# Recurrent layer's opening in a two-layer flow-matching step: two small products tied into the first units' product order, weight splits behind them, pool waits tile by tile, state copies on GpSimd

## Chip, cores, metric

One core of a Trainium2 chip runs the whole kernel. Its engines work beside each other, each through its own list of instructions in order: TensorE (PE, matrix products into PSUM), VectorE (DVE), ScalarE (ACT), GpSimd (POOL) and SyncE (SP, which only issues transfers). An instruction may wait for a semaphore that another engine raises; everything behind it on its engine then waits too. The metric is the device time of one launch in microseconds, median over runs.

## What is computed

Two layers over 512 latent and 128 context tokens of width 1024, in fp32. Layer 0 mixes by attention, layer 1 by a bidirectional gated linear recurrence; each is followed by a SwiGLU FFN. Each sub-layer has an RMS norm, a shift and scale from the conditioning vector, and a gated residual. The recurrent mixer is

```python
gate, xr = jnp.split(xm @ w_in, 2, axis=-1)
xc = _centred_depthwise_conv(xr, conv_w, conv_b)          # width 4
r = sigmoid(xc @ w_a + b_a); i = sigmoid(xc @ w_i + b_i)  # block diagonal, 8 blocks of 128, each direction
log_a = -LRU_C * r * softplus(-lam)
a, b = exp(log_a), sqrt(-expm1(2.0 * log_a)) * (i * xc)
h[t] = a[t] * h[t-1] + b[t]                               # forward and backward; latents start from state_h
y = (hs_f + hs_b) * gelu(gate)
return y @ w_out, jnp.stack([hT_f, hT_b], axis=1)         # context's last states are an output
```

with `xm = norm(x) * (1 + scale) + shift` per token.

## The kernel before

**Tiling.** Activations lie feature-major: 8 tiles of 128 features by 640 tokens. Each value and weight is split into a high part (the matmul format) and a low rest, and every product is done as three: hi·hi, hi·lo, lo·hi (L213, L214, L215). A unit is one 128-feature column of a weight. `unit` loads it to `raw` (SP, L167), makes the high part `whi` and the low part `wlo` (the split on DVE, L182). In the recurrent layer `whi` is loaded a second time by a GpSimd transfer (L178) that converts it; elsewhere ACT casts it (L180). `chunk` does one unit's 24 products (8 of k, three each) for a stretch of tokens, into a PSUM bank with the tag `mm`, of which there are three.

**Stages.** Modulation columns and first norm; attention; `ffn0` (output projection, FFN of layer 0, ending in `project_closing`); `lru`; `ffn1`. Each stage is a `phase`, which opens a pool of SBUF tiles and one of PSUM tiles in the memory that the last stage's pools held. In what order the instructions of one engine stand is decided when the program is built: a scheduler takes the program in order of writing and moves instructions within what data and buffers allow. `issue_after` ties an instruction behind another one.

**The end of ffn0.** `project_closing` does the FFN's down projection for tokens 0:384 (first chunk) of all features, then 384:640 (second chunk). Each is added to x (L436, DVE), squared (L375, ACT) and summed (L377, DVE; `self.sq` is the last). `moment` sums over the features with products against ones (L389, L392, tile `at`, per block of 128 tokens), DVE takes the variance (L394), GpSimd the power −1/2 (L396), DVE spreads it on a diagonal `dg` (L398). `spread` turns `dg` into the row factor of all partitions (L406, tile `rr`). `modulate` makes the normed input: `nv` (L411, DVE), its high part (L412, ACT), its low part (L413, DVE), tile `big`. For the first chunk this is done beside the second chunk's products, for the second chunk at the stage's end, in eight tiles.

**The recurrent layer.** Weight columns f = 0 to 7 give xr, others the gates. The opening loads x0, g0 and x1 (unit f = 0 of xr and of the gate, and unit 1 of xr) and does their first chunks, then x0's second: `x0[0], g0[0], x1[0], x0[1], g0[1]`. ACT copies xr out of PSUM (L1001); as there are three banks, x0's second chunk waits for the copies of its first. Then, in a loop over t that works on several units at once: `lru_a` does the convolution (L1009 on ACT, three L1011 on DVE), the gate products `gp` (L1021, PE), tanh (L1022, ACT) and L1023; `lru_b` does L1029, the exponential and tanh (L1033, L1034), the square root (L1035, ACT), and L1036 and L1037 (DVE); `lru_c` does four scans (L1046, DVE; two for each direction), copies the last context state out of each direction into `st` (L1048, ACT), and adds the directions (L1053, L1054); `lru_d` multiplies with the gate (L1058) and splits the result (L1062 on ACT, L1063 on DVE). The gate's unit goes through L1071, L1073 and L1075 (ACT). At the end SP writes `st` to the output `nh`.

Of the kernel before, what the change touches and what calls it, by code (L numbers as in the profile page):

```python
# [17 lines left out]
KT = D // P  # L18
# [4 lines left out]
CHL = ((0, 384), (384, 640))  # L23
# [98 lines left out]
def _pieces(t0, t1):  # L122
    return [(s, max(a, t0), min(b, t1)) for s, a, b in ((0, 0, NLAT), (1, NLAT, NTOK)) if max(a, t0) < min(b, t1)]


class _Step:
# [23 lines left out]

    @contextmanager
    def phase(self, name, **tags):
        with self.tc.tile_pool(name="ps" + name, bufs=1, space=bass.MemoryType.PSUM) as self.pp, \
                self.tc.tile_pool(name=name, bufs=1) as self.sb:
            self.wx, self.quota = [tags.pop(t, 0) for t in ("wx", "quota")]
            self.ptags, self.pbufs, self.share = list(tags), tags, True
            yield self.sb
# [45 lines left out]
                t1 = NTOK  # L203
            evac(t0, slice(t0, t1), ps[:, 0:t1 - t0])

    def chunk(self, u, xhi, xlo, t0, t1, mx=True):
        nc = self.nc
        hi, lo = u
        nk = hi.shape[1]
        ps = self.pg(mx)[:, :t1 - t0]  # L210
        s = slice(t0, t1)
        for k in range(nk):
            nc.tensor.matmul(ps, hi[:, k], xhi[:, k, s], start=(k == 0), stop=False)  # L213
            nc.tensor.matmul(ps, hi[:, k], xlo[:, k, s], start=False, stop=False)  # L214
            nc.tensor.matmul(ps, lo[:, k], xhi[:, k, s], start=False, stop=(k == nk - 1))  # L215
        return ps
# [237 lines left out]
    def project_closing(self, w, hi, lo, gk, key, nh, nl, xd):  # L454
        G = self.need(self.gcols, gk)
        A, B = [self.need(self.AB, key + (j,)) for j in range(2)]
        us = []

        def out(f, t0, t1):
            self.residual(f, t0, t1, self.chunk(us[f], hi, lo, t0, t1), G, True)  # L460
            self.nc.sync.dma_start(xd[f * P:f * P + P, t0:t1], self.x[:, f, t0:t1])

        def normed(k, t0, t1):
            v = self.t([P, 384], F32, "nv", 3, self.sb)
            for s, a, b in _pieces(t0, t1):
                self.modulate(k, a, b, A[:, s, k:k + 1], B[:, s, k:k + 1], v[:, a - t0:b - t0], nh, nl)
        for f in range(KT):
            us.append(self.unit(w[f]))
            for c, (t0, t1) in enumerate(CHL):
                if c == 0 or f < KT - DEH:  # L470
                    out(f, t0, t1)
        for c, (t0, t1) in enumerate(CHL):
            for f in range(KT - DEH, KT) if c else ():
                out(f, t0, t1)
                j = f - KT + DEH
                for k in range(max(0, 2 * j - 2), 2 * j) if f < KT - 1 else ():
                    normed(k, *CHL[0])
            self.stat(t0, t1)
        for k in range(KT):
            normed(k, *CHL[1])  # L480
# [253 lines left out]
    def normed(self, k, t0, t1, key):  # L734
        nc = self.nc
        A, B = [self.need(self.AB, key + (j,)) for j in range(2)]
        for s, a, b in _pieces(t0, t1):
            v = self.x[:, k, a:b]
            nc.vector.scalar_tensor_tensor(v, v, A[:, s, k:k + 1], self.rt[:, a:b], ALU.mult, ALU.mult)
            nc.scalar.activation(v, v, AF.Identity, bias=B[:, s, k:k + 1])  # L740
# [244 lines left out]
        c = CI["ba0"] * KT  # L985
        nc.vector.tensor_scalar(self.hb, self.cols[:, c:c + 4 * KT], 0.5, None, ALU.mult)

    def halves(self, w, hi, lo, ev):
        u = self.unit(w)
        return [lambda t0=t0, t1=t1: ev(t0, self.chunk(u, hi, lo, t0, t1)) for t0, t1 in CHL]  # L990

    def lru_xr(self, f, hi, lo):
        xr = self.xrs[f % 2]
        nat = xr[:, 2:514].rearrange("p (r c) -> p c r", r=ROWS)

        def ev(t0, ps):
            for o, a, b, r in ((nat[:, 56:64], 0, 64, ROWS), (nat[:, 0:40], 64, 384, ROWS),
                               (nat[:, 40:56], 384, 512, ROWS), (xr[:, 517:645], 512, 640, 0)):
                if t0 <= a and b <= t0 + 384:
                    v = ps[:, a - t0:b - t0]  # L1000
                    self.nc.scalar.copy(o, v.rearrange("p (c r) -> p c r", r=r) if r else v)  # L1001
        return self.halves(self.i["wi"][KT + f], hi, lo, ev)

    def lru_a(self, f, lp):
        nc, xr = self.nc, self.xrs[f % 2]
# [34 lines left out]
    def lru_c(self, f, a, h):  # L1040
        nc = self.nc
        for d in range(2):
            st = self.st[:, d * KT + f:d * KT + f + 1]
            for sl, init in ((slice(0, NLAT), self.col(f"h{d}", f)), (slice(C0, LW), 0.0)):
                hv, av = [t[:, d, sl] if d == 0 else t[:, d, sl][:, ::-1] for t in (h, a)]
                nc.vector.tensor_tensor_scan(hv, av, hv, init, ALU.mult, ALU.add)  # L1046
            e = LW - 1 if d == 0 else C0
            nc.scalar.copy(st, h[:, d, e:e + 1])  # L1048
# [13 lines left out]
        self.nc.scalar.copy(hi, v)  # L1062
        self.nc.vector.tensor_tensor(lo, v, hi.bitcast(F32), ALU.subtract)  # L1063

    def lru_gate(self, f, hi, lo, lp):
# [10 lines left out]
        return G, self.halves(self.i["wi"][f], hi, lo, ev)  # L1076

    def new_x(self, st):
        pool = st.enter_context(self.tc.tile_pool(name="x", bufs=1))
        self.x = self.t([P, KT, NTOK], F32, "x", 1, pool)  # L1080

    def load_x(self, src):
# [3 lines left out]
    def run(self):  # L1086
        nc, tc, i, o = self.nc, self.tc, self.i, self.o
# [19 lines left out]
        xhi = self.big()  # L1107
        xlo = self.big()
# [38 lines left out]
        xhi = self.big(n=NTOK + 2)  # L1147
        xlo = self.big(n=NTOK + 2)
# [12 lines left out]
        xhi, xlo = self.nh, self.nl  # L1161
# [3 lines left out]
        with self.phase("lru", at=1) as lp:  # L1165
            A, B, C, G = {}, {}, {}, {}
            self.xrs = [self.t([P, 648], F32, f"xr{j}", 1, lp) for j in range(2)]
            for xr in self.xrs:
                for a, b in ((0, 2), (514, 517), (645, 648)):
                    nc.gpsimd.memset(xr[:, a:b], 0.0)  # L1170

            def gate(g):
                G[g], halves = self.lru_gate(g, xhi, xlo, lp)
# [54 lines left out]
```

## Time and profile before

| | us |
|---|---|
| median of three runs | 1554.61 |
| lowest, highest | 1553.47, 1556.66 |
| the profiled execution, whole | 1557.38 |
| its span in the trace | 1555.6 |
| its mean granted TensorE clock | 0.988 of full |
| DVE, ACT, POOL busy | 1059.7, 698.2, 216.9 |

How rows are read: a row of a timeline has the start, the duration in us, the engine, the line, the operation, output<-input with their shapes, the count of instructions put together, and in brackets the idle time of the engine before it and what ended it. Instructions of one engine overlap a little, so durations sum to more than the time between starts. A row of windows has the stretch and its length, then the busy time of PE, PE's weight loads, DVE, ACT and POOL (each with its instructions), the granted clock of TensorE, the share of the transfer engines, and GB/s. A row of the waits has the waiting engine and line, what ended the wait, the sum, the number and the longest.

### The profile page before, as it was taken

To read this page: it belongs to the slowest core of one execution; us is meant where nothing else is said; L and a number is where in the kernel's file an instruction comes from. 1 tells how busy PE (TensorE), PEld (TensorE's weight loads), DVE (VectorE), ACT (ScalarE), POOL (GpSimd) and SP (SyncE) were. 2 spreads that over 40 slices of the span, in tenths; PEclk is the share of its full clock that TensorE was granted. 3 is DMA by queue.
4 is the path that set the end of the run, shared out by engine and by line. 5 is a ranking of instruction groups with operands and counts; after the bars stand their busy time and mean duration, and the time that the engine had idled before them with its cause. 6 is when DMAs were issued, how large, how long until landed. Compare 5 with 4: busy or idle time off the path is not lost. (4 is left out here: it accounts for less than half of the span.)

```text
span 1555.6 us, 26009 instructions
## 1 busy us (share of the span) xinstructions
PE 1491.8 (96%) x10309; PEld 1444.3 (93%) x10309; DVE 1059.7 (68%) x2000; ACT 698.2 (45%) x1282; POOL 216.9 (14%) x253
## 2 busy tenths in 40 slices
PE   6999999989999999999999799979999999999997
PEld 4899899879999999999999787779999999999996
DVE  5668788949999997434444669874875666555656
ACT  4576667655333123312332378762734342524242
POOL 2101122100111110000000000000222222222210
PEclk9999999999999999999999899999999999999998
DMA  9445656536666664222223343315242322222211
GB/s 376 146 126 158 176 159 183 145 106 190 190 191 190 191 215 130 61 82 82 68 71 101 104 153 95 115 55 200 86 136 72 92 82 81 84 79 83 81 55 68
DMA packets 73210, 196.65 MB, mean 126 GB/s; under 512 B 8176, under 2 KB 25728, under 8 KB 72960
## 3 DMA queue, kind: packets, MB, share of 16 engines
q1 hardware_dynamic: 58976, 144.49, 29.8%
q0 software_dynamic: 13824, 50.34, 10.7%
q8 instruction: 81, 1.33, 0.4%
q14 instruction: 41, 0.34, 0.1%
q10 hardware_dynamic: 288, 0.16, 0.0%
HBM read 179.48 MB, written 8.92 MB: 121 GB/s over the span
## 5 line engine op out<-in xcount | busy, mean ns | idle before, releaser
L213 PE MATMUL mm<-big,whi 128*128 128x320 f32 (+3 forms) x1290 | 402.4, 315 | 21.3 <-ACT xr L1001 9.4
L214 PE MATMUL mm<-big,whi 128*128 128x320 f32 (+3 forms) x1290 | 404.8, 314 | 0.7 <-DVE big L1063 0.4
L215 PE MATMUL mm<-big,wlo 128*128 128x320 f32 (+3 forms) x1290 | 404.0, 314 | 0.7 <-DVE wlo L182 0.7
L213 PEld LDWEIGHTS mm<-big,whi 128*128 128x128 f32 x1290 | 245.9, 192 | 26.2 <-ACT xr L1001 9.6
L214 PEld LDWEIGHTS mm<-big,whi 128*128 128x128 f32 x1290 | 247.0, 191 | 4.0 <-DVE big L1063 2.5
L215 PEld LDWEIGHTS mm<-big,wlo 128*128 128x128 f32 x1290 | 246.7, 191 | 2.2 <-DVE wlo L182 1.1
L243 DVE SCALAR_TENSOR_TENSOR mprod<-mraw,csb 128x1024 f32<-128x1024 f32 x160 | 196.2, 1226 | 13.9 <-DMA mraw<-in_wm 13.6
L436 DVE SCALAR_TENSOR_TENSOR x<-mm,G,x 128x128 f32<-128x128 f32 (+3 forms) x211 | 85.6, 436 | 94.0 <-PE mm L215 93.3
L182 DVE TENSOR_TENSOR wlo<-raw,whi 128x1024 fp32r<-128x1024 f32 (+1 forms) x90 | 110.1, 1223 | 29.8 <-ACT whi L180 21.6
L180 ACT CAST whi<-raw 128x1024 fp32r<-128x1024 f32 (+1 forms) x74 | 76.7, 1036 | 108.1 <-PE mm L214 66.5
L213 PE MATMUL mm<-big,whx 128*128 128x320 f32 (+3 forms) x363 | 113.3, 312 | 0.0
L215 PE MATMUL mm<-big,wlx 128*128 128x320 f32 (+3 forms) x363 | 113.0, 311 | 0.0
L214 PE MATMUL mm<-big,whx 128*128 128x320 f32 (+3 forms) x363 | 112.7, 311 | 0.0
L239 POOL DMA_DIRECT2D mraw<-in_wm x80 | 43.5, 544 | 385.8 <-DVE mprod L243 269.4
L213 PE MATMUL mx<-big,whi 128*128 128x320 f32 (+3 forms) x278 | 86.5, 311 | 0.9 <-DVE big L686 0.9
L214 PE MATMUL mx<-big,whi 128*128 128x320 f32 (+3 forms) x278 | 86.3, 310 | 0.0
L215 PE MATMUL mx<-big,wlo 128*128 128x320 f32 (+3 forms) x278 | 86.3, 310 | 0.0
L180 ACT CAST whx<-raw 128x1024 fp32r<-128x1024 f32 (+1 forms) x40 | 41.0, 1028 | 92.6 <-PE mm L214 55.1
L213 PE MATMUL mx<-big,whx 128*128 128x320 f32 (+3 forms) x245 | 76.0, 310 | 0.0
L215 PE MATMUL mx<-big,wlx 128*128 128x320 f32 (+3 forms) x245 | 75.7, 309 | 0.0
L214 PE MATMUL mx<-big,whx 128*128 128x320 f32 (+3 forms) x245 | 75.4, 308 | 0.0
L1062 ACT CAST whi<-raw 128x1024 fp32r<-128x1024 f32 (+1 forms) x41 | 41.4, 1009 | 72.3 <-PE mm L214 45.0
(294 smaller groups left out, 3573.5 us busy)
## 6 DMA issues: line engine op xcount, KB each, us to landing
raw<-in_gu SPq DMA_DIRECT2D x88, 512.0 KB, 3.6
mraw<-in_wm POOLq DMA_DIRECT2D x80, 512.0 KB, 4.0
raw<-in_dn SPq DMA_DIRECT2D x24, 512.0 KB, 3.7
raw<-in_wqk SPq DMA_DIRECT2D x16, 512.0 KB, 4.9
raw<-in_wi SPq DMA_DIRECT2D x16, 512.0 KB, 3.6
whi<-in_wi POOLq DMA_DIRECT2D x16, 512.0 KB, 4.1
raw<-in_dn SPq DMA_DIRECT2D x16, 448.0 KB, 3.3
sw<-in_wm SPq DMA_DIRECT2D x10, 512.0 KB, 10.6
```

The lines of the kernel that those rows point to most:

```text
L180: nc.scalar.copy(hi, raw)
L182: nc.vector.tensor_tensor(lo, raw, hi.bitcast(F32), ALU.subtract)
L213: nc.tensor.matmul(ps, hi[:, k], xhi[:, k, s], start=(k == 0), stop=False)
L214: nc.tensor.matmul(ps, hi[:, k], xlo[:, k, s], start=False, stop=False)
L215: nc.tensor.matmul(ps, lo[:, k], xhi[:, k, s], start=False, stop=(k == nk - 1))
L239: nc.gpsimd.dma_start(w, self.i["wm"][l * 6 + j - 2, f])
L243: nc.vector.scalar_tensor_tensor(prod, w, 1.0, self.csb[:, s], ALU.mult, ALU.mult, accum_out=out[:, s, f:f + 1])
L436: self.nc.vector.scalar_tensor_tensor(xs, ps[:, a - t0:b - t0], G[:, s, f:f + 1], xs, ALU.mult, ALU.add)
L1062: self.nc.scalar.copy(hi, v)
```

## The change

The two phase pools and the pool of x are opened with `reuse_waits="tile"`: a tile placed in the memory of an earlier pool waits for the tiles that lay in its own place, and not for the whole earlier pool. In the recurrent layer's opening the products of x0's first chunk from k = 3 on are tied behind the last `at` product, and g0's first product behind the last `rr` product. The low split of g0 is tied behind the last sum of squares, that of x1 behind `dg`. Two norm tiles (k = 6 and 7 of the first chunk) stand behind the last feature's residual, and are tied behind the last sum. The state copies go from ACT to GpSimd, the output transfer of the states from SP to GpSimd.

```diff
-        with self.tc.tile_pool(name="ps" + name, bufs=1, space=bass.MemoryType.PSUM) as self.pp, \
-                self.tc.tile_pool(name=name, bufs=1) as self.sb:
+        with self.tc.tile_pool(name="ps" + name, bufs=1, space=bass.MemoryType.PSUM, reuse_waits="tile") as self.pp, \
+                self.tc.tile_pool(name=name, bufs=1, reuse_waits="tile") as self.sb:
...
+    def pin(self, ins):
+        return self.tc.issue_after(ins) if ins is not None else nullcontext()
...
+    def chunk(self, u, xhi, xlo, t0, t1, mx=True, pins={}):
...
         for k in range(nk):
-            nc.tensor.matmul(ps, hi[:, k], xhi[:, k, s], start=(k == 0), stop=False)
+            with self.pin(pins.get(k)):
+                nc.tensor.matmul(ps, hi[:, k], xhi[:, k, s], start=(k == 0), stop=False)
...
         def normed(k, t0, t1):
             v = self.t([P, 384], F32, "nv", 3, self.sb)
-            for s, a, b in _pieces(t0, t1):
-                self.modulate(k, a, b, A[:, s, k:k + 1], B[:, s, k:k + 1], v[:, a - t0:b - t0], nh, nl)
+            with self.pin(self.sq if t0 == 0 and k > 5 else None):
+                for s, a, b in _pieces(t0, t1):
+                    self.modulate(k, a, b, A[:, s, k:k + 1], B[:, s, k:k + 1], v[:, a - t0:b - t0], nh, nl)
...
-                for k in range(max(0, 2 * j - 2), 2 * j) if f < KT - 1 else ():
+                for k in range(max(0, 2 * j - 2), 2 * j) if f < KT - 2 else ():
                     normed(k, *CHL[0])
+            for k in (6, 7) if c else ():
+                normed(k, *CHL[0])
             self.stat(t0, t1)
...
-    def halves(self, w, hi, lo, ev):
-        u = self.unit(w)
+    def halves(self, w, hi, lo, ev, after=None):
+        u = self.unit(w, None, after)
...
-            nc.scalar.copy(st, h[:, d, e:e + 1])
+            nc.gpsimd.tensor_copy(st, h[:, d, e:e + 1])
...
-        pool = st.enter_context(self.tc.tile_pool(name="x", bufs=1))
+        pool = st.enter_context(self.tc.tile_pool(name="x", bufs=1, reuse_waits="tile"))
...
-            x0, g0, x1 = self.lru_xr(0, xhi, xlo), gate(0), self.lru_xr(1, xhi, xlo)
-            for step in (x0[0], g0[0], x1[0], x0[1], g0[1]):
+            x0, g0, x1 = self.lru_xr(0, xhi, xlo), gate(0, self.sq), self.lru_xr(1, xhi, xlo, self.dg)
+            x0[0](pins={3: self.at})
+            g0[0](pins={0: self.rr})
+            for step in (x1[0], x0[1], g0[1]):
                 step()
...
-            nc.sync.dma_start(o["nh"], self.st)
+            nc.gpsimd.dma_start(o["nh"], self.st)
```

(`lru_xr` and `lru_gate` take the argument `after` too and hand it to `halves`.) The names in the listings below have numbers that tell one tile from the next of its kind.

On PE, around the product `rr`: before, at the end of x1's first chunk (mm_1616) and ahead of x0's second (mm_1617):

```order
L213 MATMUL mm_1616_9567<-big_1517_8871,whi_1612_9510 128x384
L214 MATMUL mm_1616_9567<-big_1518_8872,whi_1612_9510 128x384
L215 MATMUL mm_1616_9567<-big_1517_8871,wlo_1613_9511 128x384
L406 MATMUL rr_1591_9416<-dg_1590_9414,ones_5_72 128x128 x2
L213 MATMUL mm_1617_9594<-big_1517_8871,whi_1605_9497 128x256
```

and now, at the end of x0's first chunk (mm_1614) and ahead of g0's first (mm_1615):

```order
L217 MATMUL mm_1614_9514<-big_1517_8871,whi_1605_9497 128x384
L218 MATMUL mm_1614_9514<-big_1518_8872,whi_1605_9497 128x384
L219 MATMUL mm_1614_9514<-big_1517_8871,wlo_1606_9498 128x384
L410 MATMUL rr_1591_9416<-dg_1590_9414,ones_5_72 128x128 x2
L217 MATMUL mm_1615_9541<-big_1517_8871,whi_1609_9504 128x384
```

So `rr` went from behind three first chunks to behind one; the four `at` products stand behind k = 2 of x0's first chunk now, and stood behind all of g0's before.

On DVE, the end of the first norm chunk and the chain to `dg` (ssq is the sum of squares, wlo_1610 the low split of g0, wlo_1613 that of x1, big_1518 the low part of the normed input). Before, the split of g0 stands some rows ahead of these:

```order
L413 SCALAR_TENSOR_TENSOR big_1518_8872<-nv_1579_9334,B10_1108_5975,big_1517_8871 128x384
L182 TENSOR_TENSOR wlo_1613_9511<-raw_1611_9508,whi_1612_9510 128x1024
L413 SCALAR_TENSOR_TENSOR big_1518_8872<-nv_1580_9338,B10_1108_5975,big_1517_8871 128x384
L377 TENSOR_TENSOR ssq_1523_8902<-ssq_1523_8902,sq_1582_9366 128x256
L411 SCALAR_TENSOR_TENSOR nv_1583_9370<-x_863_4082,A10_1023_5343,rr_1566_9202 128x384
L411 SCALAR_TENSOR_TENSOR nv_1584_9374<-x_863_4082,A10_1023_5343,rr_1566_9202 128x384
L413 SCALAR_TENSOR_TENSOR big_1518_8872<-nv_1583_9370,B10_1108_5975,big_1517_8871 128x384
L413 SCALAR_TENSOR_TENSOR big_1518_8872<-nv_1584_9374,B10_1108_5975,big_1517_8871 128x384
L394 TENSOR_SCALAR var_1588_9410<-at_1587_9405 128x2
L398 TENSOR_TENSOR dg_1590_9414<-ident_2_63,rs_1589_9412 128x256
```

and now:

```order
L417 SCALAR_TENSOR_TENSOR big_1518_8872<-nv_1580_9338,B10_1108_5975,big_1517_8871 128x384
L381 TENSOR_TENSOR ssq_1523_8902<-ssq_1523_8902,sq_1582_9366 128x256
L415 SCALAR_TENSOR_TENSOR nv_1585_9397<-x_863_4082,A10_1023_5343,rr_1566_9202 128x384
L182 TENSOR_TENSOR wlo_1610_9505<-raw_1608_9502,whi_1609_9504 128x1024
L415 SCALAR_TENSOR_TENSOR nv_1586_9401<-x_863_4082,A10_1023_5343,rr_1566_9202 128x384
L398 TENSOR_SCALAR var_1588_9410<-at_1587_9405 128x2
L417 SCALAR_TENSOR_TENSOR big_1518_8872<-nv_1585_9397,B10_1108_5975,big_1517_8871 128x384
L417 SCALAR_TENSOR_TENSOR big_1518_8872<-nv_1586_9401,B10_1108_5975,big_1517_8871 128x384
L402 TENSOR_TENSOR dg_1590_9414<-ident_2_63,rs_1589_9412 128x256
L182 TENSOR_TENSOR wlo_1613_9511<-raw_1611_9508,whi_1612_9510 128x1024
```

Both splits went from ahead of the last sum to behind it, and the variance from behind the last two low parts to ahead of them.

On GpSimd, in the middle of the recurrent layer, the loads of the converted weights (`whi`). Before, they follow one another:

```order
L178 DMA whi_1685_10098<-in_wi 128x1024
L178 DMA whi_1692_10177<-in_wi 128x1024
L178 DMA whi_1705_10265<-in_wi 128x1024
L178 DMA whi_1712_10344<-in_wi 128x1024
L178 DMA whi_1725_10432<-in_wi 128x1024
L178 DMA whi_1732_10511<-in_wi 128x1024
L178 DMA whi_1747_10618<-in_wi 128x1024
L178 DMA whi_1754_10699<-in_wi 128x1024
```

and now the state copies (lt are the scans' tiles) stand between them:

```order
L1055 COPY st_6_74<-lt_1631_9709 128x1 x2
L178 DMA whi_1712_10344<-in_wi 128x1024
L1055 COPY st_6_74<-lt_1645_9804 128x1 x2
L178 DMA whi_1725_10432<-in_wi 128x1024
L1055 COPY st_6_74<-lt_1659_9911 128x1
L178 DMA whi_1732_10511<-in_wi 128x1024
L1055 COPY st_6_74<-lt_1659_9911 128x1
L178 DMA whi_1747_10618<-in_wi 128x1024
L1055 COPY st_6_74<-lt_1679_10078 128x1 x2
L178 DMA whi_1754_10699<-in_wi 128x1024
```

More of the change, by code (lines that the diff above doesn't have):

```diff
@@ L986, in lru_prep, with lru_xr @@
         nc.vector.tensor_scalar(self.hb, self.cols[:, c:c + 4 * KT], 0.5, None, ALU.mult)
-    def halves(self, w, hi, lo, ev):
-        u = self.unit(w)
-        return [lambda t0=t0, t1=t1: ev(t0, self.chunk(u, hi, lo, t0, t1)) for t0, t1 in CHL]
-    def lru_xr(self, f, hi, lo):
+    def halves(self, w, hi, lo, ev, after=None):
+        u = self.unit(w, None, after)
+        return [lambda t0=t0, t1=t1, **kw: ev(t0, self.chunk(u, hi, lo, t0, t1, **kw)) for t0, t1 in CHL]
+    def lru_xr(self, f, hi, lo, after=None):
         xr = self.xrs[f % 2]
@@ L1001, in ev @@
                     self.nc.scalar.copy(o, v.rearrange("p (c r) -> p c r", r=r) if r else v)
-        return self.halves(self.i["wi"][KT + f], hi, lo, ev)
+        return self.halves(self.i["wi"][KT + f], hi, lo, ev, after)
     def lru_a(self, f, lp):
@@ L1063, in split, with lru_gate @@
         self.nc.vector.tensor_tensor(lo, v, hi.bitcast(F32), ALU.subtract)
-    def lru_gate(self, f, hi, lo, lp):
+    def lru_gate(self, f, hi, lo, lp, after=None):
         nc = self.nc
@@ L1170, in run, with gate @@
                     nc.gpsimd.memset(xr[:, a:b], 0.0)
[L1172 to L1176 removed]
+            def gate(g, after=None):
+                G[g], halves = self.lru_gate(g, xhi, xlo, lp, after)
+                return halves
+            x0, g0, x1 = self.lru_xr(0, xhi, xlo), gate(0, self.sq), self.lru_xr(1, xhi, xlo, self.dg)
+            x0[0](pins={3: self.at})
+            g0[0](pins={0: self.rr})
+            for step in (x1[0], x0[1], g0[1]):
                 step()
```

3 lines of the change are left out of this document (1 added, 2 removed).

## The prediction

> **What bounds the kernel now.** I read the page first (busy shares, costliest groups), then TensorE's waits by releaser, then the windows and the timelines around the long waits. Times are of the one profiled execution: span 1555.6 us, 1557.38 us in all, 0.2% over the median of 1554.61.
>
> ```profile
> PE 1491.8 (96%) x10309; PEld 1444.3 (93%) x10309; DVE 1059.7 (68%) x2000; ACT 698.2 (45%) x1282; POOL 216.9 (14%) x253
> ```
> ```profile
> PE mm L213 <- ACT xr L1001: 9.4, 1, 9.4
> PE mm L213 <- ACT big L1062: 7.4, 3, 6.3
> ```
>
> PE is the bound: 1555.6 − 1491.8 = 64 us of the span are idle, and no more than that (and any slow clock) can be won without removing products, of which the change removes none. The first row (total, number of waits, longest) is at the opening of the recurrent layer, where x0's second chunk (256 tokens) waits 9.4 us. Of the second, 6.3 us are at that layer's end.
>
> ```profile
> 858.78 0.28 PE L215 MATMUL mm<-big,wlx 128*128 128x256 f32 x1
> ...
> 860.56 0.28 PE L215 MATMUL mm<-big,wlx 128*128 128x256 f32 x1
> 860.68 0.34 PE L213 MATMUL mm<-big,whi 128*128 128x384 f32 x1
> ...
> 874.26 0.61 PE L406 MATMUL rr<-dg,ones 128*128 128x128 f32 x4
> 884.27 0.58 PE L213 MATMUL mm<-big,whi 128*128 128x256 f32 x1 [9.40 <-ACT xr L1001]
> ```
> ```profile
> 875.00:884.00 9.00, 0.00 (x0) 0.00 (x0) 8.33 (x32) 5.92 (x18) 0.27 (x6) 0.70 0.00 0
> 884.00:889.00 5.00, 4.73 (x23) 4.73 (x24) 0.00 (x0) 1.27 (x4) 0.00 (x0) 0.52 0.29 107
> ```
>
> The wait is paid twice: the granted clock (third number from the end) falls to 0.70 in the gap and stays at 0.52 while x0's second chunk runs. Before the gap PE did three first chunks (x0, g0, x1) back to back from 860.68, and rr only behind them, at 874.26. The second chunk's norm hangs on rr:
>
> ```profile
> 864.89 0.42 DVE L377 TENSOR_TENSOR ssq<-ssq,sq 128x256 f32<-128x256 f32 x1
> ...
> 866.52 1.15 DVE L413 SCALAR_TENSOR_TENSOR big<-nv,B,big 128x384 fp32r<-128x384 f32 x2 [0.16 <-ACT big L412]
> 870.10 0.16 DVE L394 TENSOR_SCALAR var<-at 128x2 f32<-128x2 f32 x1 [2.43 <-PE at L392]
> 871.15 0.42 DVE L398 TENSOR_TENSOR dg<-ident,rs 128x256 f32<-128x256 f32 x1 [0.90 <-POOL rs L396]
> 874.90 1.64 DVE L411 SCALAR_TENSOR_TENSOR nv<-x,A,rr 128x128 f32<-128x128 f32 x6 [3.33 <-PE rr L406]
> ...
> 882.20 1.13 DVE L413 SCALAR_TENSOR_TENSOR big<-nv,B,big 128x128 fp32r<-128x128 f32 x4
> ```
> ```profile
> 881.27 1.47 ACT L412 ACTIVATE big<-nv,B 128x128 fp32r<-128x128 f32 x4 [0.87 <-DVE nv L411]
> 883.40 0.81 ACT L1001 COPY xr<-mm 128x64 f32<-128x64 f32 x2 [0.66 <-DVE big L413]
> ...
> 889.43 0.50 ACT L1001 COPY xr<-mm 128x128 f32<-128x128 f32 x2 [4.16 <-PE mm L215]
> ```
> ```profile
> 870.41 0.71 POOL L396 TENSOR_TENSOR rs<-var,mhalf 128x2 f32<-128x2 f32 x1 [11.09 <-DVE var L394]
> 883.44 0.27 POOL L1170 MEMSET xr<- 128x2 f32 x6 [12.31 <-DVE big L413]
> ```
>
> DVE waits 2.43 us for the at products and 3.33 us for rr, which stand behind other units in PE's queue though their data were there. Then eight tiles of norm, to 883.3, and only then the first xr copies: x0's first chunk lies finished in its PSUM bank since 865, but the copy's wait, like the memset's, ends with the last L413.
>
> **The change, part 1: the opening.** By the new order the g0 split no longer stands ahead of the last sum of squares, and the x1 split stands behind dg. A split holds DVE 1.14 us, so the sum of 864.89 ends near 862.6 (f = 6's square is there by 862.3). PE does k = 0 to 2 of x0 (nine products of 0.175 us from 860.68, to 862.25), waits some 0.4 us, does at in 0.8 us, and then k = 3 to 7 (15 × 0.175 = 2.6 us) to 866.1 or a little later, since the low parts for k = 6 and 7 now end near 866.1. Beside that DVE does two nv, the g0 split between them, var at 864.8, GpSimd the power (0.71 us) to 865.8, DVE two low parts (1.15 us), dg to 866.5. rr runs at 866.7, ending at 867.3. DVE uses the time for the x1 split (866.5 to 867.65), so the eight tiles start at 867.65 instead of 874.90: **7.25 us earlier**, at their old 8.4 us. ACT's last L412 (882.74 before) ends near 875.5, and the copies start there rather than after memset and last L413: 0.6 us more. x0's second chunk starts at 884.27 − 7.9 = 876.3.
>
> What is late next? PE has g0's and x1's first chunks as cover: 48 × 0.175 = 8.4 us from 867.3, to 875.6. A gap of 0.7 us is left. Whether the clock drops in it is read from other gaps:
>
> ```profile
> 986.40:988.60 2.20, 0.12 (x1) 0.00 (x0) 2.20 (x3) 1.93 (x3) 0.00 (x0) 1.00 0.00 0
> 988.60:990.60 2.00, 1.99 (x6) 1.09 (x7) 2.00 (x2) 1.27 (x4) 0.00 (x0) 1.00 0.00 0
> ```
> ```profile
> 1047.40 0.90 PE L213 MATMUL mm<-big,whi 128*128 128x320 f32 x2 [6.27 <-ACT big L1062]
> ```
> ```profile
> 1047.40:1051.00 3.60, 3.60 (x13) 3.51 (x14) 2.44 (x3) 2.66 (x3) 0.00 (x0) 0.50 0.19 37
> ```
>
> After 2.1 us without products the clock is still 1.00; after 6.27 us it is 0.50. So with gaps under 1 us it should hold. The chunk took 5.1 us (884.27 to the copies at 889.43); at the pitch of the 256-wide products before the gap (1.78 us for 15, 0.119 each) 24 take 2.85. I take 2.0 us of the difference. Opening: −7.9 − 2.0 = **−9.9 us**, between −7.9 (the clock falls all the same) and −10.5. It carries through, since xc of unit 0 and all scans follow x0's second chunk.
>
> The Trainium skill, "TensorE: Matmul & The Clock Gate", section "What's actually happening", gives half clock after an idle window of about 3.4 us, and full clock after as long a busy one, the window running freely. By that rule a gap of 0.7 us leaves the clock alone, and the two rows above agree; the sum would be the same, and if the gap were several microseconds some 2 us less.
>
> **Part 2: the state copies.** Sixteen copies of one column each leave ACT for GpSimd.
>
> ```profile
> L1048 ACT COPY st<-lt x16: 177/192/216, 932.6 to 1042.2; 128x1 f32<-128x1 f32 x16
> its engine sat idle before it (us, times) until:
>   DVE lt L1046: 14.8, 11
> ```
> ```profile
> 925.00:979.00 54.00, 51.28 (x299) 43.98 (x298) 52.93 (x63) 46.57 (x70) 3.26 (x5) 1.00 0.37 115
> ```
> ```profile
> 974.33 0.19 ACT L1048 COPY st<-lt 128x1 f32<-128x1 f32 x1 [2.04 <-DVE lt L1046]
> 975.83 0.19 ACT L1048 COPY st<-lt 128x1 f32<-128x1 f32 x1 [1.30 <-DVE lt L1046]
> ```
> ```profile
> 971.83 1.24 PE L1021 MATMUL gp<-xc,gw 128*128 128x512 f32 x4
> ```
> ```profile
> 986.26 1.50 DVE L1036 SCALAR_TENSOR_TENSOR lt<-lt,lt 128x1286 f32<-128x1286 f32 x1 [1.36 <-ACT lt L1035]
> ...
> 1006.19 1.50 DVE L1036 SCALAR_TENSOR_TENSOR lt<-lt,lt 128x1286 f32<-128x1286 f32 x1 [2.26 <-ACT lt L1035]
> ...
> 1028.55 2.91 DVE L1036 SCALAR_TENSOR_TENSOR lt<-lt,lt 128x1286 f32<-128x1286 f32 x2 [1.77 <-ACT lt L1035]
> ```
>
> ACT stands 14.8 us in these waits for a scan, with tanh, exp and square root queued behind. Until 979 that costs nothing: DVE is busy 52.93 of 54 us and is the bound. After it DVE waits for ACT's square root (L1035) each round. Walking ACT's queue without the copies: the tanh held up behind the pair at 974 and 975 starts when its gate product is there (971.83 + 1.24 = 973.07) and not behind the second copy, at 975.92, so L1035 and the L1036 of 986.26 come 2.85 us earlier; the next pair (994, 995) lets the L1036 of 1006.19 come 4.85 us earlier, the pair at 1011 and 1013 the one of 1028.55 6.3 us. From there DVE runs without a gap to 1047, so the layer's last values, for which PE waits 6.27 us up to 1047.40, move as a whole. I take **−6.0**, between 0 and −6.5.
>
> A copy's price on GpSimd isn't in this trace. The nearest rows are a memset (0.27 us for six) and the power (0.71 us), so 16 cost 0.7 to 11 us of an engine that is 14% busy. What queues behind them there are the whi loads:
>
> ```profile
> 929.89 0.53 POOL L178 DMA_DIRECT2D whi<-in_wi  x1 [11.29 <-DVE xc L1011]
> ...
> 972.29 0.53 POOL L178 DMA_DIRECT2D whi<-in_wi  x1 [8.99 <-DVE wlo L182]
> ...
> 993.13 0.53 POOL L178 DMA_DIRECT2D whi<-in_wi  x1 [11.06 <-PE mm L215]
> ```
> By the new order these three stand behind a copy that waits for a scan (for the second of them the copy that stood at 974.33), 2 to 3 us each. Their splits move by about 1 us, into time that DVE spent waiting for ACT (1.36 and 2.26 us above, before L1036). If that cover were gone, they would take back 1 to 3 us. The state's output transfer goes from SP's queue to GpSimd's and is issued there behind the last copy, with no load behind it for which PE waits: nothing.
>
> The Trainium skill, "SBUF — State Buffer", section "Who interferes with whom", speaks against this part: a DVE instruction with two SBUF inputs and a GpSimd one that reads SBUF lock each other out. By it each copy may hold a scan or product of DVE for its whole length; with the two rows above that would give back 0.7 to 11 us of the sum. No row of before shows the two side by side.
>
> **Part 3: tile-wise pool waits elsewhere.** At the attention's end
>
> ```profile
> 345.00 1.23 DVE L243 SCALAR_TENSOR_TENSOR mprod<-mraw,csb 128x1024 f32<-128x1024 f32 x1 [3.11 <-DMA mraw<-in_wm]
> ```
> ```profile
> 346.98 0.38 PE L213 MATMUL mm<-big,whi 128*128 128x320 f32 x1 [0.84 <-DVE x L436]
> ```
> DVE waits for an mraw load that was issued only when attention's last product was done; it now waits for an earlier one, some 2 us before. PE can win its 0.84 us: **−0.8** (0 to −1.2). The other phase boundaries show no such wait of PE: 0.
>
> **Sum:** −9.9 − 6.0 − 0.8 = −16.7, so 1557.4 → 1540.7 for the profiled execution, and 1554.6 − 16.7 = **1538 us** on the median.
>
> **The rivals.**
> 1. *The copies win little.* DVE is the bound in the layer (52.93 of 54 us), and late whi loads or slow copies take the rest. For it: three loads queue behind copies. Against: the three waits of DVE for L1035. Then −9.9 − 0.8 − 1.0: about 1543.
> 2. *The opening wins less.* x0's products stall on the tied chain so that g0 and x1 end later, or the clock falls anyway: half of the 9.9 is left, 1543; with rival 1 too, 1548.
> 3. *The boundary still waits.* If the copies still wait for the last L413, with PE in order behind them, only the 7.25 us is won, less what fills; with all tile waits void and the pins without effect, the copies alone are left: about 1548 to 1554, nearly no change.
> 4. *Slower: the ties themselves.* PE works in order, so x0's k = 3 waits for the sum of squares, and g0 for rr, with nothing ahead of them as cover but 2.6 us of products, where before 8.4 us stood there. If var or dg are stuck behind norm tiles and splits on DVE, PE stands twice. Price: each stall its own length, and about 2.2 us more where it is long enough to drop the clock (6.27 us does). It decides from two stalls of over 8 us together beyond the cover and no win from the copies (−9.9 − 0.8 used up), giving 1558 to 1560. Against: DVE's rows ahead of dg sum to under 5 us.
>
> **How the numbers follow.** Forecast (1534 to 1541.5): 0.60. Rival 1 (1541 to 1546): 0.17. Rival 2 (1541 to 1548): 0.12. Rival 3 (1548 to 1556): 0.06. Rival 4 (over 1557.7): 0.03. Better than all bounds (under 1534): 0.02. A measurement tells 0.2%, 3.1 us, from no change. The bounds sum to −18.2 at best, 1536.4, and with the spread between executions (1553.47 to 1556.66) 1533; on the other side rivals 1 and 2 go in: 1533 to 1547. Faster 0.93, same 0.04, slower 0.03.
>
> **What would show it.** Opening: rr near 867, nv tiles from about 867.7, the wait of x0's second chunk under 1 us, clock 1.00 throughout. If PE shows new waits over 1 us at x0's k = 3 or g0's first product, rival 2 or 4. Copies: DVE's waits for L1035 gone or shorter, the layer's end 16 to 17 us earlier; if DVE instead waits for whi loads, rival 1. ACT's xr copies still released by the last L413: rival 3. The forecast is wrong where PE's idle sum (64 us) doesn't fall by some 14 us.

## The result, and the profile after

| | before | changed |
|---|---|---|
| median, us (4 runs each) | 1554.04 | 1538.35 |
| lowest to highest | 1552.91 to 1556.66 | 1537.96 to 1539.57 |
| span of the profiled execution | 1555.6 | 1536.3 |

Ratio 0.9898, 95% interval 0.9881 to 0.9915: 15.7 us faster. The forecast was 1538, in a range of 1533 to 1547. The sum was near; two of its three terms were mis-sized, and their errors nearly cancelled, as the traces show.

Line numbers move with the change: L213 to L215 become L217 to L219, the copies of xr L1008, L1011 L1018, L1021 and L1022 L1028 and L1029, L1035 and L1036 L1042 and L1043, the scans L1053, the state copies L1055, L1062 and L1063 L1069 and L1070.

The changed kernel's opening, on PE and on DVE (columns as before):

```profile
856.92 0.38 PE L393 MATMUL at<-ones,ssq 128*128 128x1 f32 x2 [0.35 <-DVE ssq L381]
...
860.87 0.66 PE L410 MATMUL rr<-dg,ones 128*128 128x128 f32 x4
...
870.36 0.38 PE L217 MATMUL mm<-big,whi 128*128 128x256 f32 x1 [0.37 <-ACT xr L1008]
```
```profile
860.28 0.42 DVE L402 TENSOR_TENSOR dg<-ident,rs 128x256 f32<-128x256 f32 x1
860.62 1.22 DVE L182 TENSOR_TENSOR wlo<-raw,whi 128x1024 fp32r<-128x1024 f32 x1
861.75 1.63 DVE L415 SCALAR_TENSOR_TENSOR nv<-x,A,rr 128x128 f32<-128x128 f32 x6
```
```profile
862.00:870.00 8.00, 7.99 (x46) 7.66 (x44) 8.00 (x32) 5.75 (x18) 0.00 (x0) 1.00 0.23 68
870.00:874.00 4.00, 3.64 (x30) 3.64 (x31) 0.17 (x1) 1.87 (x6) 0.35 (x1) 1.00 0.43 131
```

The execution came to the opening 5.84 us earlier than the one of before; with that added, rr starts at 866.71 (forecast 866.7), the second chunk's norm at 867.59 (867.65), x0's second chunk at 876.20 (876.3). Its wait is 0.37 us where it was 9.40, and the windows' third column from the end shows the clock at 1.00 through it. The copies of xr no longer wait for the last low part, which runs beside them (ACT, then DVE):

```profile
868.12 1.48 ACT L416 ACTIVATE big<-nv,B 128x128 fp32r<-128x128 f32 x4 [0.88 <-DVE nv L415]
869.50 0.81 ACT L1008 COPY xr<-mm 128x64 f32<-128x64 f32 x2
```
```profile
869.04 1.13 DVE L417 SCALAR_TENSOR_TENSOR big<-nv,B,big 128x128 fp32r<-128x128 f32 x4
```

The recurrent layer behind it is another matter. First GpSimd's timeline in the changed kernel, then DVE's:

```profile
917.02 6.74 POOL L1055 COPY st<-lt 128x1 f32<-128x1 f32 x1
...
958.81 1.34 POOL L1055 COPY st<-lt 128x1 f32<-128x1 f32 x1 [10.70 <-DVE lt L1053]
960.09 0.93 POOL L178 DMA_DIRECT2D whi<-in_wi  x1
...
978.72 1.99 POOL L1055 COPY st<-lt 128x1 f32<-128x1 f32 x1 [0.47 <-DVE lt L1053]
980.65 0.53 POOL L178 DMA_DIRECT2D whi<-in_wi  x1
```
```profile
965.14 1.23 DVE L182 TENSOR_TENSOR wlo<-raw,whi 128x1024 fp32r<-128x1024 f32 x1 [2.87 <-issue]
...
969.29 1.49 DVE L1043 SCALAR_TENSOR_TENSOR lt<-lt,lt 128x1286 f32<-128x1286 f32 x1
...
984.65 1.23 DVE L182 TENSOR_TENSOR wlo<-raw,whi 128x1024 fp32r<-128x1024 f32 x1 [2.26 <-DMA whi<-in_wi]
...
988.00 1.49 DVE L1043 SCALAR_TENSOR_TENSOR lt<-lt,lt 128x1286 f32<-128x1286 f32 x1
...
1008.94 2.91 DVE L1043 SCALAR_TENSOR_TENSOR lt<-lt,lt 128x1286 f32<-128x1286 f32 x2 [1.77 <-ACT lt L1042]
```

DVE no longer waits for ACT's square root ahead of the first two of these L1043. Two weight splits wait for their whi instead, 2.87 and 2.26 us: the loads were issued at 960.09 and 980.65, each time right behind a state copy. (The first bracket names no releaser. Of the loads ahead of that split the last of raw was issued at 956.46 and landed by 961.5, the whi at 960.09 by 965.1.)

PE runs the same 10309 products in every kernel here, so the starts of chosen products in its order cut the span into comparable stages. "Opening" runs from the 5980th product (just ahead of x0) to the 6150th, "layer" from there to the 7050th (some way into ffn1):

| us, one profile each | attention's end (2463rd to 2560th) | opening | layer |
|---|---|---|---|
| before | 16.2 | 35.9 | 168.4 |
| changed | 14.0 | 25.8 | 163.9 |
| gain (forecast) | 2.2 (0.8) | 10.1 (9.9) | 4.5 (6.0) |

The three sum to 16.8; 1.1 us is given back behind the layer. The rest of the 19.3 between the two spans lies ahead of attention's end, and goes with no edit (last section). One profile is not exact: a second one of the changed kernel (change_again, below) has 14.0, 25.7 and 163.1, so the layer's gain is 4.5 to 5.3 us.

### The profile page after: what moved, and what is told of

The parts are those of the page before. It is cut to its first block, busy times and chain, and to the rows that moved or that the text cites. A ratio compares the mean times of both kernels' runs of the same rounds, so it can differ in the third digit from the quotient of the medians.

```text
span 1536.3 us, 25993 instructions
## 1 busy us (share of the span) xinstructions
PE 1483.2 (97%) x10309; PEld 1437.0 (94%) x10309; DVE 1060.9 (69%) x2000; ACT 695.3 (45%) x1266; POOL 253.2 (16%) x270
## 5 line engine op out<-in xcount | busy, mean ns | idle before, releaser
L217 PE MATMUL mm<-big,whi 128*128 128x320 f32 (+3 forms) x1290 | 400.1, 313 | 9.0 <-ACT big L1069 7.3
L219 PE MATMUL mm<-big,wlo 128*128 128x320 f32 (+3 forms) x1290 | 401.9, 312 | 1.9 <-DVE wlo L182 1.6
L217 PEld LDWEIGHTS mm<-big,whi 128*128 128x128 f32 x1290 | 243.6, 190 | 13.5 <-ACT big L1069 8.2
L219 PEld LDWEIGHTS mm<-big,wlo 128*128 128x128 f32 x1290 | 244.4, 190 | 3.7 <-DVE wlo L182 2.1
L217 PE MATMUL mm<-big,whx 128*128 128x320 f32 (+3 forms) x363 | 113.3, 312 | 0.0
L219 PE MATMUL mm<-big,wlx 128*128 128x320 f32 (+3 forms) x363 | 113.0, 311 | 0.0
L217 PE MATMUL mx<-big,whi 128*128 128x320 f32 (+3 forms) x278 | 86.6, 311 | 0.0
L219 PE MATMUL mx<-big,wlo 128*128 128x320 f32 (+3 forms) x278 | 86.3, 310 | 0.0
L217 PE MATMUL mx<-big,whx 128*128 128x320 f32 (+3 forms) x245 | 75.8, 309 | 0.0
L219 PE MATMUL mx<-big,wlx 128*128 128x320 f32 (+3 forms) x245 | 75.6, 309 | 0.0
L1069 ACT CAST whi<-raw 128x1024 fp32r<-128x1024 f32 (+1 forms) x41 | 41.3, 1008 | 72.8 <-PE mm L218 45.1
## 6 DMA issues: line engine op xcount, KB each, us to landing
sw<-in_wm SPq DMA_DIRECT2D x10, 512.0 KB, 10.1
```

## The experiments

Each was timed in five rounds beside the kernel before on the same chip. The stages come from each run's profile, cut as above.

| run | median, us | ratio to before (95%) | attention's end | opening | layer |
|---|---|---|---|---|---|
| copies_back | 1543.99 | 0.9936 (0.9923 to 0.9948) | 14.2 | 25.8 | 167.8 |
| copies_only | 1550.35 | 0.9978 (0.9965 to 0.9991) | 16.5 | 35.7 | 164.8 |
| copies_late | 1535.68 | 0.9881 (0.9867 to 0.9896) | 14.2 | 25.8 | 161.2 |
| no_tile_waits | 1542.49 | 0.9921 (0.9905 to 0.9937) | 16.4 | 26.5 | 165.3 |
| no_product_ties | 1546.02 | 0.9950 (0.9937 to 0.9962) | 15.0 | 31.7 | 163.0 |
| product_ties_only | 1544.70 | 0.9946 (0.9930 to 0.9962) | 15.0 | 30.5 | 166.5 |
| tile_waits_only | 1553.38 | 0.9991 (0.9978 to 1.0004) | 14.1 | 34.9 | 168.1 |
| copies_twice | 1544.27 | 0.9941 (0.9929 to 0.9952) | 14.5 | 25.7 | 167.6 |
| late_copies_only | 1546.90 | 0.9947 (0.9931 to 0.9963) | 16.5 | 36.0 | 161.7 |
| change_again | 1539.52 | 0.9904 (0.9886 to 0.9921) | 14.0 | 25.7 | 163.1 |
| copies_late_again | 1534.78 | 0.9872 (0.9853 to 0.9890) | 14.8 | 25.7 | 161.4 |

**The copies back on ACT, and the copies alone.** The edits undo the last two hunks of the change, or make only these:

```diff
-            nc.gpsimd.tensor_copy(st, h[:, d, e:e + 1])
+            nc.scalar.copy(st, h[:, d, e:e + 1])
...
-            nc.gpsimd.dma_start(o["nh"], self.st)
+            nc.sync.dma_start(o["nh"], self.st)
```

> The change with the state copies back on ScalarE and the output transfer of the states back on SyncE, the rest as changed. Theory (the copies' waits held up ScalarE's queue and with it DVE): slower than the change by 4.4 us (what the two traces show in the layer) to 6.0 (the prediction's term), so 1542.7 to 1544.4, with DVE waiting for the square root again. Rival (copies of 1 to 6.7 us on GpSimd, and weight loads behind them, give the gain back, and the opening is all): within 1 us of the change, 1537.5 to 1539.5.

> The kernel before with only the state copies on GpSimd and the output transfer of the states on GpSimd's queue. Theory: 4.4 to 6.0 us under before (1554.0), so 1548.0 to 1549.6, opening gap of 9.4 us as before. Rival (it gives nothing): 1553 to 1555.

With the copies back the time is 1544.0, as the theory has it. DVE's waits for the square root are back too: 2.5 us in two waits in the change, and now (the copies_back kernel, waits of DVE around the layer):

```profile
DVE lt L1043 <- ACT lt L1042: 6.6, 4, 2.3
```

Counted from the start of the layer's stage, the three L1043 of the listings stand at 93.3, 113.3 and 135.6 us, just as in the kernel before, and at 92.3, 111.0 and 132.0 in the change.

With the copies alone it is 1550.4, 3.3 us under before, less than expected, though the layer's stage in its trace is 3.6 us shorter. So the copies on GpSimd are worth something; the medians put it at 3.3 to 5.6 us.

**The copies on ACT, but later.** Here the copies go back to ACT, tied behind the cast of the same unit's result, which waits for the scans in any case:

```diff
     def lru_c(self, f, a, h):
...
-            nc.gpsimd.tensor_copy(st, h[:, d, e:e + 1])
+            self.ends.append((st, h[:, d, e:e + 1]))
...
     def lru_d(self, f, y, G, yhi, ylo):
+        y, ends = y
         self.nc.vector.tensor_tensor(y, y, G, ALU.mult)
-        self.split(yhi[:, f], ylo[:, f], y)
+        hi, lo = yhi[:, f], ylo[:, f]
+        last = self.nc.scalar.copy(hi, y).ins
+        self.nc.vector.tensor_tensor(lo, y, hi.bitcast(F32), ALU.subtract)
+        for st, e in ends:
+            with self.tc.issue_after(last):
+                self.nc.scalar.copy(st, e)
```

> The change with the state copies on ScalarE again, but each pair placed behind the cast of the same unit's result (where its scan is long done), output transfer back on SyncE. Theory (what the copies on GpSimd still cost are DVE's two waits for weight loads behind them, 2.9 and 2.3 us): faster than the change by 2 to 5 us, 1533.5 to 1536.5, and no wait of ScalarE ahead of a copy. Rival (something else bounds the layer, DVE's own work or PE): 1537.5 to 1539.5.

> The kernel before with only the state copies moved: still on ScalarE, each pair behind the cast of its unit's result. Theory (a copy harms by its place in ScalarE's queue, not by the engine it is on): the recurrent layer behind its opening takes about 161 us instead of 168.4, so 1546 to 1548.5; opening gap 9.4 us as before. Rival (without the opening's gain the layer is bound elsewhere): 1549 to 1552.

> The change itself, beside the next one on the same chip: 1537 to 1540.

> The change with the state copies on ScalarE behind the cast of the unit's result, once more, beside the change on the same chip. Theory: 2 to 3.5 us under it (2.7 in the layer by the traces so far). Rival (the first comparison fell apart by chance between chips): within 1 us of it.

1535.7, then 1534.8 beside 1539.5 for the change on the same chip (1533.5 to 1536.8 against 1537.1 to 1544.0: no overlap). That is 4.7 us, more than the 2 to 3.5 expected, and more than the layer shows: 1.7 us between the traces of these two runs, 2.7 between copies_late and the first trace of the change. On the kernel before it takes off 8.1 us (1554.95 to 1546.90; 6.7 in the layer's stage). In the trace of copies_late neither the wait for the scans nor that for whi is left in this stretch; ACT first, then DVE:

```profile
956.48 0.28 ACT L1073 COPY st<-lt 128x1 f32<-128x1 f32 x2
...
973.62 0.28 ACT L1073 COPY st<-lt 128x1 f32<-128x1 f32 x2
```
```profile
969.92 1.50 DVE L1043 SCALAR_TENSOR_TENSOR lt<-lt,lt 128x1286 f32<-128x1286 f32 x1 [1.35 <-ACT lt L1042]
987.65 1.50 DVE L1043 SCALAR_TENSOR_TENSOR lt<-lt,lt 128x1286 f32<-128x1286 f32 x1 [1.28 <-ACT lt L1042]
...
1008.18 2.91 DVE L1043 SCALAR_TENSOR_TENSOR lt<-lt,lt 128x1286 f32<-128x1286 f32 x2 [1.77 <-ACT lt L1042]
```

The copies have no idle time ahead of them (no bracket), and cost 0.28 us a pair. The whi loads whose splits waited are issued 3.2 and 5.3 us earlier than in the change, counted from the stage's start. What harmed on ACT was the copies' place in its queue, not the engine. This version is the fastest of all.

**Each copy twice on GpSimd.**

```diff
             nc.gpsimd.tensor_copy(st, h[:, d, e:e + 1])
+            nc.gpsimd.tensor_copy(self.st2[:, d * KT + f:d * KT + f + 1], h[:, d, e:e + 1])
```

> The change with each state copy on GpSimd done twice (the second into a tile that nothing reads), the same order on the other engines. Theory (the copies cost by the weight loads queued behind them, DVE itself is not held): slower than the change by 1 to 4 us, 1539.4 to 1542.5, DVE's waits for the weight loads longer by 1 to 2 us each, DVE's busy sum the same within 2 us. Rival (each copy also holds DVE for its length, 1 us or more): DVE's busy sum 16 us up, time over 1545. Second rival (the copies cost nothing): 1538 to 1539.

1544.3: slower than the change by 4.8 to 5.9 us between medians (the change was measured twice), 3.7 in the layer's stage, more than the 1 to 4 expected. The waits for whi are longer than the 2.87 and 2.26 above (copies_twice, DVE's timeline):

```profile
967.30 1.23 DVE L182 TENSOR_TENSOR wlo<-raw,whi 128x1024 fp32r<-128x1024 f32 x1 [4.16 <-PE mm L219]
...
987.53 1.23 DVE L182 TENSOR_TENSOR wlo<-raw,whi 128x1024 fp32r<-128x1024 f32 x1 [2.97 <-DMA whi<-in_wi]
```

DVE's busy sum is 1060.6 us, against 1060.9 in the change: DVE is not held by the copies, and the first rival falls. How much the second copies cost is less clear. These two waits vary between executions with single copies as well: 1.35 and 2.15 us in change_again, 4.04 and 2.89 in product_ties_only. And some 1.6 us of the stage is no wait for whi: the clock is at half from 989.4 to 992.8, where it stays at 1.00 in the change, and DVE waits 2.43 us for L1029 behind it, where the change waits 0.88 (the tile-wise waits, below, show the same). That the loads behind the copies are what costs rests on the comparison with copies_late: in all seven executions with the copies on GpSimd these splits wait, 1.29 us or more, and in the three with late copies on ACT they don't.

**The opening without the ties on PE, and without those on DVE.**

```diff
-            x0[0](pins={3: self.at})
-            g0[0](pins={0: self.rr})
+            x0[0]()
+            g0[0]()
```

> The change without the two ties on PE (x0's k = 3 behind at, g0's first product behind rr); the splits stay tied. PE then has at 13 products later in its order and rr 26 products later. Theory (rr's place sets the opening): the second chunk's norm starts 26 x 0.175 = 4.5 us later than in the change, the gap of x0's second chunk is about 5 us, and the clock falls in it for up to 2 us more: 1542.5 to 1545. Rival (tying the splits alone is enough): 1537.5 to 1539.5.

```diff
-            x0, g0, x1 = self.lru_xr(0, xhi, xlo), gate(0, self.sq), self.lru_xr(1, xhi, xlo, self.dg)
+            x0, g0, x1 = self.lru_xr(0, xhi, xlo), gate(0), self.lru_xr(1, xhi, xlo)
```

> The change without the ties of the two weight splits (both stand ahead of the last sum of squares on DVE again); the same order on PE as the change. Theory: at comes up to two splits (2.3 us) later and var stands behind two low parts, while the x1 split is no longer ahead of the second chunk's norm (1.1 us): slower than the change by 1.2 to 2.3 us, 1539.5 to 1540.7, gap of x0's second chunk 1.5 to 2.7 us with the clock still at 1.00. Rival (PE's order alone sets it): 1537.5 to 1539.

Without the ties on PE: 1546.0. rr stands 2.8 us later than in the change's trace, in an execution that came to the opening 0.9 us earlier, so 3.7 us behind its place (expected: 4.5), and x0's second chunk waits (PE of no_product_ties):

```profile
863.64 0.61 PE L410 MATMUL rr<-dg,ones 128*128 128x128 f32 x4
...
872.89 0.58 PE L217 MATMUL mm<-big,whi 128*128 128x256 f32 x1 [4.76 <-ACT xr L1008]
```

The wait is as expected, about 5 us; the clock falls too, as the first product's 0.58 us for 0.38 shows, and the stage costs 5.9 us more. The time is 1 us above the 1542.5 to 1545 expected.

Without the ties of the splits: 1544.7, outside what was expected. The splits do delay the sum of squares by about two of their lengths, but PE now stands in its tied order at x0's k = 3, as the fourth rival had it, and the clock falls (PE, then windows, of product_ties_only):

```profile
861.93 0.58 PE L393 MATMUL at<-ones,ssq 128*128 128x1 f32 x2 [2.56 <-DVE ssq L381]
...
868.54 0.61 PE L410 MATMUL rr<-dg,ones 128*128 128x128 f32 x4
...
877.82 0.38 PE L217 MATMUL mm<-big,whi 128*128 128x256 f32 x1 [0.21 <-ACT xr L1008]
```
```profile
856.00:861.60 5.60, 3.37 (x25) 3.06 (x23) 5.60 (x13) 2.04 (x4) 0.27 (x1) 1.00 0.72 234
861.60:868.40 6.80, 6.47 (x23) 6.47 (x24) 2.97 (x7) 1.14 (x2) 0.93 (x7) 0.50 0.25 80
```

A wait of 2.56 us was enough for 6.8 us at half clock, and so rr is late after all. (The layer's stage of this trace is 2.6 us longer too, with the longer waits for whi given above; that is not put down to the ties.) The two kinds of ties win the opening together: without either, 4.7 to 5.9 of the 10.1 us are gone.

**The tile-wise waits.** Taken out of the change, and put alone into the kernel before; the order on every engine stays in both:

```diff
-        with self.tc.tile_pool(name="ps" + name, bufs=1, space=bass.MemoryType.PSUM, reuse_waits="tile") as self.pp, \
-                self.tc.tile_pool(name=name, bufs=1, reuse_waits="tile") as self.sb:
+        with self.tc.tile_pool(name="ps" + name, bufs=1, space=bass.MemoryType.PSUM) as self.pp, \
+                self.tc.tile_pool(name=name, bufs=1) as self.sb:
...
-        pool = st.enter_context(self.tc.tile_pool(name="x", bufs=1, reuse_waits="tile"))
+        pool = st.enter_context(self.tc.tile_pool(name="x", bufs=1))
```

> The change without the tile-wise pool waits (the two phase pools and the pool of x wait as before), the same order of instructions on every engine. Theory (the order won the opening, the waits only the start of the copies 0.6 us earlier and the boundary after attention 0.8 to 2.0): slower than the change by 1.4 to 2.6 us, 1539.8 to 1541.0. Rival (the tile-wise waits won the opening): 1546 to 1548.

> The kernel before with only the tile-wise pool waits, the same order on every engine. Theory: 2.1 us at the boundary after attention and 0.6 to 0.9 at the opening: 1550.7 to 1551.5, with x0's second chunk still waiting 8.5 to 8.8 us. Rival (the tile-wise waits give the opening): 1544 to 1546.

Without them 1542.5, 1.5 us above what was expected: the stages show 2.4 us at attention's end, 0.7 at the opening, near what the theory has, and 1.4 in the layer, which it doesn't have. Those 1.4 are the clock. In this execution it is at half for 3.4 us from 991.7 on, so the products that L1029 reads come later and DVE waits longer for it (no_tile_waits, a window and DVE; then DVE of the change):

```profile
991.70:995.20 3.50, 3.50 (x10) 2.55 (x10) 3.47 (x3) 1.59 (x2) 0.00 (x0) 0.51 0.34 137
```
```profile
1004.86 1.50 DVE L1030 SCALAR_TENSOR_TENSOR lt<-lt,xc 128x1286 f32<-128x1286 f32 x1 [2.47 <-ACT lt L1029]
```
```profile
999.67 1.50 DVE L1030 SCALAR_TENSOR_TENSOR lt<-lt,xc 128x1286 f32<-128x1286 f32 x1 [0.88 <-ACT lt L1029]
```

Alone they give 1553.4, not to be told from no change by time, and missing the 1550.7 to 1551.5 expected; in the trace they give 2.1 us at attention's end and 1.0 at the opening. x0's second chunk waits on (PE of tile_waits_only):

```profile
879.70 0.58 PE L213 MATMUL mm<-big,whi 128*128 128x256 f32 x1 [8.64 <-ACT xr L1001]
```

So the rival by which the waits won the opening falls.

## Why the forecast held, step by step

**The opening: right in size and in mechanism.** 10.1 us for 9.9, of which 8.1 are there at the second chunk's start (forecast 7.9) and 2.0 come behind it (2.0 for the clock). rr, the norm and the second chunk stand within 0.1 us of the forecast's places, and the gap that was to be 0.7 us is 0.37. That the order did it, and not the waits, is shown by no_tile_waits (26.5 us for the stage against 25.8). The clock term is shown by the changed kernel's windows: 1.00 where it was 0.52.

**The copies: the right mechanism, mis-sized.** The term was −6.0 us, measured −4.5 between the first two profiles and −5.3 with the second one of the change. The walk along ACT's queue was sound: in copies_late, where nothing takes its place, the three L1043 are 2.2, 4.4 and 6.3 us earlier than before once the earlier opening (14.1 us between these two executions) is taken off; the walk had 2.85, 4.85 and 6.3. With the copies on GpSimd they are 1.0, 2.3 and 3.7 us earlier (15.9 us taken off). The step that failed is that the whi loads' delay goes "into time that DVE spent waiting for ACT": two of the splits waited 2.87 and 2.26 us, and DVE with them (1.35 and 2.15 in change_again). The forecast had a price for it, "1 to 3 us" if that cover were gone, and 1.9 to 2.7 us is what copies_late wins back in the stage over the change's two traces. Why the cover was too small can be read in part: the forecast let the splits move by about 1 us, and their loads are issued 3.2 and 5.3 us later than in copies_late. The copies right ahead of them took 1.34 and 1.99 us of GpSimd, where its nearest rows were 0.27 us for six memsets and 0.71 for the power; the longest of the sixteen took 6.7. So the first rival's mechanism was real, but not its size: it left 1.0 us of the term.

The Trainium skill, "SBUF — State Buffer", section "Who interferes with whom", bears on these lengths: a DVE instruction with two SBUF inputs and a GpSimd one that reads SBUF exclude each other. The traces fit that, with GpSimd as the side that waits: the longest copy, 6.74 us, stands beside DVE instructions with two tensors that follow each other without a gap, and the scans take 1272 ns on average where they took 1278 (before, then changed):

```profile
L1046 DVE TENSOR_TENSOR_SCAN lt<-lt,cols,lt 128x512 f32<-128x512 f32 x16 | 20.5, 1278 | 0.0
```
```profile
L1053 DVE TENSOR_TENSOR_SCAN lt<-lt,cols,lt 128x512 f32<-128x512 f32 x16 | 20.4, 1272 | 0.0
```

That the lock is what makes the copies long is argued from this, not shown by a run; spans on GpSimd are rough in any case.

**Attention's end: too small.** 0.8 us forecast, 2.2 measured (2.1 in tile_waits_only). The forecast read one wait of PE there, the 0.84 us for L436. The one 10 us ahead of it, at the first product of the output projection, went too (kernel before, PE):

```profile
337.21 0.39 PE L213 MATMUL mx<-big,whi 128*128 128x320 f32 x1 [0.95 <-DVE big L686]
```

So the sum came out by luck: this term was 1.4 us too small and the copies' 0.7 to 1.5 too large.

**The rest of the rivals.** The second, that the opening wins less, falls with the 10.1 us. The third, that the boundary still waits, is refuted by the first xr copy, which starts at 869.50, while the last low parts run from 869.04 to 870.17. The fourth, slower by the ties, did not come in the change, but its mechanism is real: product_ties_only is it, with one stall of 2.56 us in place of the two of over 8 us together that would have turned the sign. Not taken apart were the two norm tiles tied behind the last sum, which stood in every run made from the change, and the output transfer, which moved together with the copies.

**The sign that came out against it.** The forecast called itself wrong where PE's idle sum doesn't fall by some 14 us. It fell by 10.7: from 1555.6 − 1491.8 = 63.8 us to 1536.3 − 1483.2 = 53.1. In the three stages it fell by 1.8, 8.7 and 4.5, 15.0 together, as meant; but 3.6 us of idle time came on ahead of attention's end and 0.7 behind the layer, where no edit reached. Over a whole execution the sign was a poor one, since it takes in what differs between any two executions.

## What to carry to other kernels

A small instruction that waits for another engine costs its queue the wait, whichever queue it is put into: before moving it to an idle engine, list what is queued behind it there (here loads of weights), and look first for a place in its old queue where its input is long done. When one tie makes an engine wait in order, tie the work ahead of what it waits for as well; with either kind of tie alone only about half of the opening's gain was left. A sum that comes out right is no proof of its terms: compare stage by stage.

## What was not expected of the hardware

**The clock's fall is not a matter of the wait's length alone.** The same wait of PE, for the same L1029 (L1022 before), was 1.88 us before, where the clock stayed at 1.00, and 1.86 us in the change, where it fell (PE, then windows, of the kernel before; then the same of the changed kernel):

```profile
940.58 1.35 PE L1021 MATMUL gp<-xc,gw 128*128 128x512 f32 x4 [1.88 <-ACT lt L1022]
```
```profile
936.60:940.00 3.40, 2.09 (x18) 1.89 (x16) 3.40 (x4) 3.37 (x5) 0.00 (x0) 1.00 0.00 0
940.00:943.40 3.40, 2.82 (x12) 1.87 (x13) 3.40 (x5) 2.65 (x4) 1.06 (x1) 1.00 0.52 159
```
```profile
924.62 1.46 PE L1028 MATMUL gp<-xc,gw 128*128 128x512 f32 x4 [1.86 <-ACT lt L1029]
```
```profile
922.30:925.70 3.40, 1.54 (x8) 0.86 (x8) 3.40 (x5) 2.92 (x4) 1.46 (x1) 1.00 0.22 33
925.70:929.10 3.40, 3.40 (x11) 2.36 (x10) 3.40 (x4) 2.96 (x4) 0.93 (x1) 0.50 0.41 146
```

What differs is where the wait lies. In the clock records of each of the 13 traces, all changes of the granted clock after the first 60 us are whole multiples of 3.41 us apart, as if on one grid through the execution; stretches at half clock between products last 3.4, 6.8 or 10.2 us. In the change the wait lies within one cell of that grid, 922.3 to 925.7, in which PE is busy for only 1.54 of 3.40 us, and the next cell is at half clock. Before, the grid line at 940.0 cuts the wait in two, and both cells stay busier, 2.09 and 2.82 us. Over the 13 traces, again after the first 60 us and with the ends of products as the profile models them, no cell at full clock with PE idle for less than 44% of it was followed by a fall, and every one with more than 54% was.

What a fall costs depends on where it comes. copies_late has one at 927.9 and copies_late_again has none in the layer, and the stage takes 161.2 and 161.4 us; the one in no_tile_waits cost 1.4.

The forecast's sentence that 2.1 us leave the clock alone was true of the gap that it quoted, which the grid line at 987.8 cuts, and not in general; the opening's 0.37 us is a ninth of a cell. The Trainium skill, "TensorE: Matmul & The Clock Gate", section "What's actually happening", has a window that runs freely, and the grid agrees with it; that a window must be idle for about 3.4 us does not agree with falls behind 1.86 and 2.56 us.

**Two profiles differ by chance.** Of the 19.3 us between the spans, 3.6 lie ahead of attention's end (the 2463rd product starts at 335.7 before and at 332.0 in the change), where PE's order is the same in both. The stretch from the 1250th to the 2463rd product takes 155.3 to 155.5 us in five of the profiled executions and 152.8 to 153.7 in the other eight, with kernels of both kinds in each group: the longer ones have a half-clock stretch of 6.8 us at 300. No edit goes with it. The first 1250 products take 174.1 to 177.8 us, again without regard to the edit. The 1.1 us behind the layer is of this size too: from the 7050th product to the end the 13 executions take 493.9 to 496.7 us, kernels of both kinds mixed. At attention's end the kernels with tile-wise waits take 14.0 to 15.0 us; the three at 14.8 to 15.0 are the ones in which the half-clock stretch that reaches up to it lasts 6.8 us, and not 3.4.
